# Second-norm shift summed into columns, priority for weight casts, a ninth place for mixer weights, fewer transfers at the opening

## The chip, the core and the metric

One NeuronCore of a Trainium2 chip. The time is the device time of one execution in microseconds (us); the kernel before has a median of 1503.98 us over three runs (1502.64 to 1508.92). Everything is float32 in HBM. The engines are TensorE (PE, its weight loads PEld), VectorE (DVE), ScalarE (ACT), GpSimd (POOL) and SyncE (SP), which here only issues transfers.

## The reference, cut to what matters

A trunk of two layers over 256 tokens of width 1024. Each layer is a mixer (an mLSTM branch and an attention branch, merged and projected) and a mixture of 32 experts of which each token uses two.

```python
for l in range(DEPTH):                                   # 2
    mod = silu(c) @ w_ada[l] + b_ada[l]                  # (1, 6144): six vectors of 1024
    shift1, scale1, gate1, shift2, scale2, gate2 = split(mod, 6)
    h = rms_norm(x, norm1_g[l]) * (1 + scale1) + shift1
    proj = h @ w_in[l] + b_in[l]                         # 1024 x 4880
    ...                                                  # conv, mLSTM, rotary attention, gates
    merged = sigmoid(gm) * (y_m @ w_branch_m[l]) + sigmoid(ga) * (y_a @ w_branch_a[l])
    x = x + gate1 * (merged @ w_out[l])
    h2 = rms_norm(x, norm2_g[l]) * (1 + scale2) + shift2
    x = x + gate2 * hierarchical_moe(h2, ...)            # router, then 32 experts of 3 x 2 MB
return rms_norm(x, final_norm_g)
```

The change turns on `shift2`. It enters twice: as a bias of the router's logits (`shift2 @ w_router`), and as a bias that is added to the gathered tokens of each expert.

## The kernel before, in words

**Weights.** All large weights come in pieces of 1 MB (half a block of 512 columns of `w_in` or `w_ada`, or half an expert matrix) through one list, `plan`, that SP works off in order (`pump`, L151). A piece is sent when a place for it is free. The places are slots of 8 KB per partition: in the mixer four slots of the arena (0, 1, 2, 15) and three tiles `y`, so seven (`usual`), and at the opening of layer 0 four more for `w_ada` alone (`ONCE`). Other slots of the arena hold the mixer's data; late in the mixer they are released one after the other (`free:7:13:14` in the order, L1023, L1078, L1115), and then expert weights go to them too. During the experts all 16 slots and more take expert weights.

**Casts.** The mixer's matmuls run in three passes over operands split into a rounded high part (fp32r) and the rest. For each half block of 256 columns, `prep` (L488) takes a weight piece, casts it on ACT (L495, 128x1024), and subtracts half on DVE and half on POOL (L496, L497, inside `low`, L477). The result goes to one of two spare tiles (three from the merge on). `dense` (L502) first issues the casts for which a spare tile is free, and then 24 matmuls of 256 columns (L535, L550, L523) on the oldest cast weights.

**Order.** PE and SP run in the order of the program (`manual_schedule`). The string `MIX[l]` gives it: a number is so many steps of `dense`, a word is a piece of other work (`dec0` to `dec4` the decays of the mLSTM, `ms` and `mo` its scores and outputs, `as`, `at`, `ao` attention, `kr`, `kt`, `qr`, `qt` the rotary parts). For ACT, DVE and POOL a list scheduler decides the order at build time: among what it takes to be ready, it prefers what the program issues earlier.

**Modulation.** The words `r4` to `r11` and `c0` to `c3` are blocks of 512 columns of `w_ada`, `r` for this layer and `c` for the next. Block b of six pairs: 4, 5 are gate1, 6, 7 are shift2, 8, 9 scale2, 10, 11 gate2; in layer 0 blocks 0 to 3 (`FIRST`: shift1, scale1) open the kernel, in layer 1 blocks 4 and 5 (`EARLY`) open the mixer. `ada_part` (L405) multiplies (L410), casts the partial sums on ACT (L414) and subtracts on DVE (L415); one dense step later `finish` calls `ada_row`, whose two matmuls against a matrix of ones (L442) sum over the partitions and repeat the sum on all 128 of them; DVE adds that to a row tile which holds the bias (L465). For shift2 the row tile is `sh2b`, loaded as a broadcast of 512 KB (L234).

**Where shift2 is turned.** In the middle of the merge, L1062 to L1072 turn one row of `sh2b` into columns: 8 matmuls with one contraction row and two columns (`psh`, L1064; each shows as two records) for the router, with index k outermost, and 8 (`psj`, L1069) with a strided weight read for the experts, with k innermost. L1081 then multiplies the columns with the router weights `wr`.

**Opening.** `setup` (L342) issues `c` and `x` on ACT's queue, the eight pieces of `w_ada` for `FIRST` on SP's, and 13 transfers of small parameters (`params`, L308) on POOL's; one of these, `wg8` (L324), has 1024 runs of 64 bytes. PE then takes two blocks of `FIRST`, transposes x (L664), turns the parameters (L338), turns the blocks' sums (L435), takes the other two blocks, and starts with `dense`.

Of the kernel before, what the change touches and what calls it, by code (L numbers as in the profile page):

```python
# [43 lines left out]
FIRST = (0, 2, 1, 3)  # L44
ORDER = (("q", 2), ("k", 2), ("akv", 1), ("aq", 2), ("v", 2), ("o", 2), ("gm", 4), ("ga", 4))
# [3 lines left out]
    "3 gates 1 gates2 dec0 tables 3 dec1 1 c0 dec2 2 dec3 r5 1 dec4 2 kr 1 qr:0 r11 1 kt 2 qr:1 1 r7 1 hold qt:0 1 ms:0 1 c1 qt:1 2 ms:1 1 as:0 r8 mo:0 mo:1 2 r9 ms:3 1 ms:2 at:0 at:4 r4 as:1 mo:2 1 r10 1 at:1 mo:3 ao:0 at:5 r6 1 ao:2 as:2 mn c2 free:7:13:14 2 mt at:2 1 as:3 2 at:3 c3 at:6 at:7 ao:1 1 ao:3 2",  # L49
    "1 tables 1 gates 2 gates2 dec0 3 dec1 1 dec2 2 dec3 1 dec4 1 kr 2 kt r10 1 qr:0 2 qr:1 r6 1 hold 3 ms:0 qt:1 2 r8 ms:1 1 qt:0 mo:0 as:0 1 r9 mo:1 as:1 1 ms:2 r11 at:0 at:4 ms:3 mo:2 2 at:5 1 at:1 mo:3 ao:0 r7 ao:2 1 as:2 mn free:7:13:14 2 at:2 at:6 1 mt as:3 2 at:3 at:7 ao:1 1 ao:3 2")  # L50
# [4 lines left out]
def trunk(ctx, tc, x, c, w_ada, b_ada, norm1_g, w_in, b_in, conv_w, conv_b, mlstm_norm_g, q_norm_g, k_norm_g,  # L55
# [164 lines left out]
    A2b, sh2b = at(4, 0, D), at(4, D, D)  # L220
# [11 lines left out]
    def late_loads2(l):  # L232
        for t, o in ((g1b, 2), (sh2b, 3), (A2b, 4), (gt2b, 5))[l > 0:]:
# [4 lines left out]
    def first_params():  # L238
        first["p"] = params(0, nc.gpsimd)

    for l in range(depth):
# [5 lines left out]
        for it in stream(l):  # L247
# [60 lines left out]
    def params(l, q):  # L308
# [96 lines left out]
    def ada_part(l, b):  # L405
        pb = ps.tile([P, 512], F32, tag="f", name="pada")
        for h in range(2):
# [4 lines left out]
            done("ada", l, b, h)  # L412
        ph, pw = parts_at[0][:, 0, :], parts_at[0][:, 1, :]
        A.copy(ph, pb)  # L414
        V.tensor_tensor(pw, pb, ph.bitcast(F32), op=ALU.subtract)  # L415
        return ph, pw

    def ada_fast(b):

        pb = ps.tile([P, 512], F32, tag="f", name="pada")  # L420
        for h in range(2):
            w = wt("ada", 0, b, h)
            for kk in range(4):
                T.matmul(pb[32 * kk:32 * kk + 32, :], lhsT=condp[:, 4 * h + kk, :], rhs=w[:, kk, :],
# [1089 lines left out]
```

## Time and profile before

| | |
|---|---|
| median of runs | 1503.98 us (1502.64 to 1508.92) |
| profiled execution | 1508.72 us |
| its span on the core | 1507.0 us, 20322 instructions |
| PE busy | 1358.7 us, 90% |
| PEld, DVE, ACT, POOL busy | 797.8 (53%), 642.6 (43%), 396.0 (26%), 275.9 us (18%) |
| moved by DMA | 522.26 MB, 346 GB/s from and to HBM over the span |

By stage (span of the stage, PE busy, DMA share and rate in it):

| stage | us | PE busy | DMA share | GB/s |
|---|---|---|---|---|
| opening, 0 to 38.95 | 38.95 | 20.18 | 0.98 | 332 |
| mixer of layer 0, to 318 | 279.05 | 254.76 | 0.75 | 264 |
| experts of layer 0, to 771 | 453.00 | 419.17 | 1.00 | 413 |
| mixer of layer 1, to 1047 | 276.00 | 249.74 | 0.64 | 232 |
| experts of layer 1 and end, to 1507 | 460.00 | 414.83 | 0.97 | 401 |

A DMA share near 1 means that all 16 DMA engines of the core have work all the time. A PE that is busy in the table may be busy at half its clock; the column PEclk of the views below tells.

### The profile page before, as it was taken

To read this page: it belongs to the slowest core of one execution; us is meant where nothing else is said; L and a number is where in the kernel's file an instruction comes from. 1 tells how busy PE (TensorE), PEld (TensorE's weight loads), DVE (VectorE), ACT (ScalarE), POOL (GpSimd) and SP (SyncE) were. 2 spreads that over 40 slices of the span, in tenths; PEclk is the share of its full clock that TensorE was granted. 3 is DMA by queue.
4 is the path that set the end of the run, shared out by engine and by line. 5 is a ranking of instruction groups with operands and counts; after the bars stand their busy time and mean duration, and the time that the engine had idled before them with its cause. 6 is when DMAs were issued, how large, how long until landed. Compare 5 with 4: busy or idle time off the path is not lost. (4 is left out here: it accounts for less than half of the span.)

```text
span 1507.0 us, 20322 instructions
## 1 busy us (share of the span) xinstructions
PE 1358.7 (90%) x7902; PEld 797.8 (53%) x7903; DVE 642.6 (43%) x1396; ACT 396.0 (26%) x729; POOL 275.9 (18%) x318
## 2 busy tenths in 40 slices
PE   5899999879999989889978999997999999887996
PEld 2877779834434434334347887994434443334432
DVE  1887664632323312223258867554223323213223
ACT  2536554411111101011035366633111111101101
POOL 4644324500000000000015543550000000000000
PEclk9899999989999999989989999998999999999998
DMA  9877687769999999999995657666999999999995
GB/s 330 314 268 245 245 281 281 275 275 422 420 422 421 420 421 422 420 418 375 416 388 193 227 199 256 224 252 227 422 420 421 422 420 422 421 421 419 378 422 218
DMA packets 122633, 522.26 MB, mean 347 GB/s; under 512 B 14068, under 2 KB 16320, under 8 KB 74400
## 3 DMA queue, kind: packets, MB, share of 16 engines
q1 hardware_dynamic: 116448, 517.00, 86.4%
q0 software_dynamic: 1200, 1.99, 0.7%
q10 hardware_dynamic: 4880, 1.87, 0.5%
q8 instruction: 66, 1.08, 0.3%
q14 instruction: 39, 0.32, 0.1%
HBM read 519.77 MB, written 1.05 MB: 346 GB/s over the span
## 5 line engine op out<-in xcount | busy, mean ns | idle before, releaser
L1268 PE MATMUL pgu<-arena 128*64 128x512 f32 x1456 | 349.3, 595 | 20.5 <-DMA arena<-in_w_up_dram 12.0
L1268 PEld LDWEIGHTS pgu<-arena 128*64 128x64 f32 x1456 | 115.4, 137 | 222.8 <-issue 172.8
L1277 DVE SCALAR_TENSOR_TENSOR arena<-pgu,wsl,arena 128x512 f32<-128x512 f32 x32 | 36.4, 1137 | 383.0 <-PE pgu L1268 383.0
L1293 PE MATMUL pd<-arena 128*64 128x512 f32 x720 | 179.8, 597 | 7.3 <-ACT arena L1284 7.3
L1224 POOL TENSOR_TENSOR arena<-oh,arena 128x256 f32<-128x256 f32 x32 | 19.5, 615 | 740.9 <-DVE oh L1218 468.8
L477 POOL TENSOR_TENSOR R<-arena,R 128x512 fp32r<-128x512 f32 (+1 forms) x84 | 124.9, 1490 | 156.3 <-ACT R L495 104.4
L535 PE MATMUL pd<-R,R 128*128 128x256 f32 x1008 | 134.2, 291 | 9.0 <-DVE R L477 5.7
L550 PE MATMUL pd<-R,R 128*128 128x256 f32 x1056 | 136.4, 288 | 2.2 <-DVE R L477 1.9
L535 PEld LDWEIGHTS pd<-R,R 128*128 128x128 f32 x1008 | 127.1, 197 | 18.4 <-issue 6.9
L550 PEld LDWEIGHTS pd<-R,R 128*128 128x128 f32 x1056 | 130.6, 194 | 8.1 <-issue 4.4
L1304 DVE TENSOR_TENSOR y<-pd,arena 128x512 f32<-128x512 f32 x64 | 44.1, 691 | 204.0 <-PE pd L1293 167.7
L1268 PE MATMUL pgu<-B,arena 128*64 128x512 f32 x432 | 118.0, 594 | 2.7 <-DMA B<-in_w_up_dram 2.7
L477 DVE TENSOR_TENSOR R<-arena,R 128x512 fp32r<-128x512 f32 (+1 forms) x100 | 83.3, 840 | 58.5 <-ACT R L495 53.8
L1293 PEld LDWEIGHTS pd<-arena 128*64 128x64 f32 x720 | 56.0, 138 | 95.3 <-issue 85.5
L1305 ACT CAST yh<-y 128x512 fp32r<-128x512 f32 x64 | 39.6, 619 | 241.9 <-DVE y L1304 241.9
L495 ACT CAST R<-arena 128x1024 fp32r<-128x1024 f32 x76 | 79.4, 1046 | 80.5 <-PE pd L550 26.7
L1316 DVE TENSOR_TENSOR xs<-xs,psc 128x512 f32<-128x512 f32 x128 | 79.3, 680 | 17.9 <-PE psc L1313 17.9
L1240 PE MATMUL pG<-oh,X 128*128 128x256 f32 x512 | 74.3, 309 | 13.2 <-DVE oh L1218 9.0
L1240 PEld LDWEIGHTS pG<-oh,X 128*128 128x128 f32 x512 | 70.8, 215 | 24.2 <-issue 24.2
L1268 PEld LDWEIGHTS pgu<-B,arena 128*64 128x64 f32 x432 | 38.4, 137 | 73.2 <-issue 61.2
L1284 ACT COPY arena<-pat 128x512 f32<-128x512 f32 x32 | 18.7, 585 | 220.1 <-PE pat L1283 220.1
L1244 ACT ACTIVATE arena<-pG,sh2c 128x256 f32<-128x256 f32 x64 | 30.3, 474 | 159.0 <-DVE arena L1246 159.0
(328 smaller groups left out, 1694.4 us busy)
## 6 DMA issues: line engine op xcount, KB each, us to landing
arena<-in_w_up_dram SPq DMA_DIRECT2D x104, 1024.0 KB, 19.8
arena<-in_w_down_dram SPq DMA_DIRECT2D x90, 1024.0 KB, 19.8
arena<-in_w_gate_dram SPq DMA_DIRECT2D x78, 1024.0 KB, 19.8
arena<-in_w_ada_dram SPq DMA_DIRECT2D x36, 1024.0 KB, 6.4
B<-in_w_gate_dram SPq DMA_DIRECT2D x30, 1024.0 KB, 19.8
arena<-in_w_in_dram SPq DMA_DIRECT2D x27, 1024.0 KB, 8.2
B<-in_w_up_dram SPq DMA_DIRECT2D x24, 1024.0 KB, 19.8
X<-in_w_gate_dram SPq DMA_DIRECT2D x20, 1024.0 KB, 19.8
```

Of the source, the lines that this page charges most:

```text
L477: eng.tensor_tensor(dst, full, hi.bitcast(F32), op=ALU.subtract)
L495: A.copy(wh, w)
L535: T.matmul(acc[key][o][:, 0:S], lhsT=w[:, kk, P * o:P * o + P], rhs=x_[:, 4 * kh + kk], start=kh == 0 and i == 0 and kk == 0, stop=kh == 1 ...
L550: T.matmul(acc[key][t][:, 0:256], lhsT=x_[:, 4 * kh + kk, P * t:P * t + P], rhs=w[:, kk], start=kh == 0 and i == 0 and kk == 0, stop=kh == ...
L1240: T.matmul(pG[:, kk, 0:n], lhsT=x_[:, t, k, :], rhs=oh[:, t, :], start=i == 0, stop=i == 3)
L1244: A.activation(xg[k][:, 0:n], pG[:, kk, 0:n], AF.Identity, bias=sh2c[:, k:k + 1])
L1268: T.matmul(pg[CAP * e:CAP * e + CAP, :], lhsT=xg[4 * h + kk][:, P * (i % 2) + CAP * e:P * (i % 2) + CAP * e + CAP], rhs=w[e][:, kk, :], st ...
L1277: V.scalar_tensor_tensor(ac.rearrange("p k q -> p q k"), pu.rearrange("p (q k) -> p q k", k=4), wsl[:, 0:1], sl.rearrange("p (q k) -> p q ...
L1293: T.matmul(pd[n][CAP * e:CAP * e + CAP, :], lhsT=aT[:, 2 * h + kk, CAP * e:CAP * e + CAP], rhs=w[e][:, kk, 512 * n:512 * n + 512], start=h ...
L1304: V.tensor_tensor(y[:, cs], pd, gt2b[:, cs], op=ALU.mult)
L1305: A.copy(yh[:, cs], y[:, cs])
L1316: V.tensor_tensor(xx, xx, pq, op=ALU.add)
```

## The change

1. **Shift2 in columns.** Blocks 6 and 7 no longer go through `ada_part` and `ada_row`. `ada_shift` multiplies as before and copies the partial sums on ACT, reordered, to `turned_sums`; one step later `shift_put` sums over partitions with 8 matmuls whose weights are 64 columns of it, and adds the bias `b3`, straight into the columns `sh2c`. The broadcast of 512 KB, the `psh` and `psj` matmuls and their copies go. The router's bias uses a second copy of the router weights, `wr2`, in the order of `sh2c`, loaded on POOL's queue (runs of 16 and 128 bytes).
2. **Priority for casts.** In `prep` and `ada_part`, cast and subtractions are issued with a priority 60 instructions earlier.
3. **A further place.** A tile `z`, taken first, in each mixer, for all but expert weights and the final norm's gain.
4. **Opening.** The seven transfers of `params` that the first matmuls don't need, and `b3`, move from POOL's queue to SP's list, after the second piece of `w_in` (layer 0 alone). PE transposes x after the first block of `FIRST`, not after the second.
5. **Order.** `dec1` comes one dense step later in both layers; in layer 1 `kt` and some others shift by one too.

```diff
+PREP = 60
-    "3 gates 1 gates2 dec0 tables 3 dec1 1 c0 dec2 2 dec3 r5 1 dec4 2 kr 1 qr:0 ...
-    "1 tables 1 gates 2 gates2 dec0 3 dec1 1 dec2 2 dec3 1 dec4 1 kr 2 kt r10 1 qr:0 2 qr:1 r6 1 hold 3 ms:0 ... 2 at:5 ...
+    "3 gates 1 gates2 dec0 tables 4 dec1 1 c0 dec2 2 dec3 r5 1 dec4 1 kr 1 qr:0 ...
+    "1 tables 1 gates 2 gates2 dec0 4 dec1 1 dec2 2 dec3 1 dec4 1 kr 2 r10 1 kt qr:0 2 qr:1 r6 1 hold 2 ms:0 ... 1 at:4 ... 1 at:5 ...
@@ fits
+        if kind == "z":
+            return key[0] not in ("wg", "wu", "wd", "fin")
@@
-    A2b, sh2b = at(4, 0, D), at(4, D, D)
+    A2b = at(4, 0, D)
+    turned_sums, wr2 = at(4, D, KD, 64), at(4, D + 512, KD, 36)
-        for t, o in ((g1b, 2), (sh2b, 3), (A2b, 4), (gt2b, 5))[l > 0:]:
+        for t, o in ((g1b, 2), (A2b, 4), (gt2b, 5))[l > 0:]:
@@ the list of transfers
+            if l == 0 and it == ("q", 0, 1):
+                add(("more", l), lambda: first["p"]["more"](), None)
@@ params: br (2), wg8, gb, gqk (2) are now in more(q2)
+            b3 = sm.tile([P, KD], F32, tag="b3", name="b3", bufs=1)
+            q2.dma_start(b3, b_ada[l, 3 * D:4 * D].rearrange("(p k) -> p k", k=KD))
@@ setup
+        first_params()
         pump()
-        first_params()
@@ ada_part (ada_sums: the matmuls of L406 to L412)
-        A.copy(ph, pb)
-        V.tensor_tensor(pw, pb, ph.bitcast(F32), op=ALU.subtract)
+        with tc.high_priority(offset=PREP):
+            A.copy(ph, pb)
+            V.tensor_tensor(pw, pb, ph.bitcast(F32), op=ALU.subtract)
+    def ada_shift(l, b):
+        A.copy(turned_sums, ada_sums(l, b).rearrange("p (q k) -> p k q", k=KD))
+    def shift_put(sh2c, b3, b):
+        o = 64 * (b % 2)
+        pc = ps.tile([P, 512], F32, tag="f", name="pshift")
+        for k in range(KD):
+            T.matmul(pc[o:o + 64, 2 * k:2 * k + 2], lhsT=turned_sums[:, k, :], rhs=ones[:, 0:2], start=True, stop=True,
+                     tile_position=(0, o))
+        V.tensor_tensor(sh2c[o:o + 64, :], pc[o:o + 64, 0:2 * KD].rearrange("p (k o) -> p k o", o=2)[:, :, 0],
+                        b3[o:o + 64, :], op=ALU.add)
@@ mixer
+        tiles["z"] = [pool.tile([P, SLOT], F32, name="spare")]
+        free.insert(0, ("z", 0))
@@ prep
-            A.copy(wh, w)
-            low(wl[:, 0:2], w[:, 0:2], wh[:, 0:2], V)
-            low(wl[:, 2:4], w[:, 2:4], wh[:, 2:4], G)
+            with tc.high_priority(offset=PREP):
+                A.copy(wh, w)
+                low(wl[:, 0:2], w[:, 0:2], wh[:, 0:2], V)
+                low(wl[:, 2:4], w[:, 2:4], wh[:, 2:4], G)
@@ opening of layer 0
-            for b in FIRST[:2]:
-                fast[b] = ada_fast(b)
+            fast = {FIRST[0]: ada_fast(FIRST[0])}
         ... (x is transposed here)
             params_cols(p)
+            fast[FIRST[1]] = ada_fast(FIRST[1])
@@ row(b)
+            if b // 2 == 3:
+                ada_shift(l, b)
+                last_sum.append(lambda: shift_put(sh2c, p["b3"], b))
+                return
@@ before the loop over MIX
+        sh2c = sm.tile([P, KD], F32, tag="sh2c", name="sh2c")
+        nc.gpsimd.dma_start(wr2[:, :, 0:4], w_rg[l].rearrange("(p k) g -> p k g", k=KD))
+        nc.gpsimd.dma_start(wr2[:, :, 4:36], w_re[l].rearrange("(p k) g -> p k g", k=KD))
@@ after dense(4)
-        L1062 to L1072: psh, its copy, psj, its copy
-            T.matmul(pL[0][:, 72:108], lhsT=shT[:, k, 0:1].to_broadcast([P, P]), rhs=wr[:, k, :], ...
+            T.matmul(pL[0][:, 72:108], lhsT=sh2c[:, k:k + 1].to_broadcast([P, P]), rhs=wr2[:, k, :], ...
```

## Rows read from the trace of the kernel before

**Rows 1.** Windows: busy us (instructions) of PE, PEld, DVE, ACT, POOL, clock, DMA share, GB/s.

```profile
38.95:318.00 279.05, 254.76 (x1938) 219.39 (x1940) 190.91 (x453) 136.84 (x253) 118.57 (x120) 0.94 0.75 264
318.00:771.00 453.00, 419.17 (x1973) 175.29 (x1969) 126.06 (x212) 53.29 (x96) 9.52 (x20) 0.98 1.00 413
```

**Rows 2.** Window of 5 us where layer 0 passes from mixer to experts, same columns.

```profile
310.00:315.00 5.00, 5.00 (x29) 4.83 (x29) 1.57 (x4) 1.42 (x3) 0.00 (x0) 0.62 0.00 0
```

**Rows 3.** Waits of SP, 0 to 360 us: total us, times, longest.

```profile
SPq L168 <- PE pgu L1268: 32.3, 8, 13.6
```

**Rows 4.** Timeline of PE: start, us, engine, line, operation, output<-inputs, count [idle before <-releaser].

```profile
245.71 1.94 PE L1064 MATMUL psh<-onesr,arena 1*128 1x2 f32 x16
247.52 3.94 PE L1069 MATMUL psj<-onesr,arena 1*128 1x2 f32 x16
251.38 5.04 PE L523 MATMUL pm<-Y,R 128*128 128x256 f32 x24
...
259.14 5.91 PE L523 MATMUL pm<-Y,R 128*128 128x256 f32 x48
```

**Rows 5.** Windows of 5 us in which the clock falls, both mixers.

```profile
65.00:70.00 5.00, 4.26 (x29) 4.26 (x30) 4.78 (x8) 3.05 (x6) 2.89 (x5) 0.80 0.70 228
195.00:200.00 5.00, 5.00 (x21) 2.16 (x24) 1.92 (x5) 0.37 (x1) 0.00 (x0) 0.50 0.02 6
250.00:255.00 5.00, 5.00 (x24) 4.99 (x24) 1.10 (x3) 0.00 (x0) 0.17 (x1) 0.50 0.31 80
850.00:855.00 5.00, 5.00 (x31) 4.91 (x31) 4.28 (x18) 1.05 (x1) 2.00 (x3) 0.69 0.31 85
```

**Rows 6.** Groups by line and shape, whole span: busy, mean ns | idle before, releasers.

```profile
L435 PE MATMUL pcol<-onesr,arena 128*128 128x2 f32 x32 | 3.8, 250 | 0.0
L442 PE MATMUL prow<-part,onesr 128*128 128x512 f32 x40 | 14.9, 430 | 7.6 <-DVE part L415 7.0 <-ACT part L414 0.6
L535 PE MATMUL pd<-R,R 128*128 128x256 f32 x1008 | 134.2, 291 | 9.0 <-DVE R L477 5.7 <-ACT R L495 3.1 <-POOL R L477 0.2
L550 PE MATMUL pd<-R,R 128*128 128x256 f32 x1056 | 136.4, 288 | 2.2 <-DVE R L477 1.9 <-DVE arena L465 0.3
L410 PE MATMUL pada<-arena,condp 128*32 128x512 f32 x248 | 33.4, 644 | 2.9 <-DMA arena<-in_w_ada_dram 2.9
L495 ACT CAST R<-arena 128x1024 fp32r<-128x1024 f32 x76 | 79.4, 1046 | 80.5 <-PE pd L550 26.7 <-PE pd L535 16.9 <-PE pm L523 16.4
```

**Rows 7.** Timeline of PE around the sum of block 6, layer 0.

```profile
191.28 0.39 PE L442 MATMUL prow<-part,onesr 128*128 128x512 f32 x1
...
194.55 0.79 PE L442 MATMUL prow<-part,onesr 128*128 128x512 f32 x1 [2.88 <-DVE part L415]
```

**Rows 8.** Timeline of ACT, DVE and PE at 58 to 66 us.

```profile
58.73 1.03 ACT L495 CAST R<-arena 128x1024 fp32r<-128x1024 f32 x1
60.73 4.27 DVE L567 SCALAR_TENSOR_TENSOR arena<-arena,cols 128x256 f32<-128x256 f32 x8
65.74 1.22 PE L535 MATMUL pd<-R,R 128*128 128x256 f32 x8 [2.58 <-DVE R L477]
```

**Rows 9.** Window in which the convolution runs, layer 0.

```profile
60.00:125.00 65.00, 56.91 (x431) 47.57 (x430) 58.90 (x147) 24.82 (x34) 29.54 (x38) 0.97 0.74 253
```

**Rows 10.** Waits of PE, 700 to 1100 us: the decays of layer 1.

```profile
PE pb L747 <- DVE lf L742: 2.2, 1, 2.2
```

**Rows 11.** Timeline of PE at the opening.

```profile
33.60 1.04 PE L424 MATMUL pada<-arena,condp 128*32 128x512 f32 x8
...
38.95 11.14 PE L535 MATMUL pd<-R,R 128*128 128x256 f32 x72 [2.44 <-ACT R L495]
```

**Rows 12.** Windows of 5 us: small parameters at 10, large pieces at 25, router weights at 220.

```profile
10.00:15.00 5.00, 0.84 (x4) 0.20 (x8) 0.76 (x6) 1.17 (x3) 3.52 (x17) 1.00 0.93 244
25.00:30.00 5.00, 5.00 (x39) 5.00 (x37) 0.26 (x1) 0.00 (x0) 0.35 (x1) 1.00 1.05 387
220.00:225.00 5.00, 5.00 (x42) 2.87 (x42) 4.79 (x6) 4.38 (x7) 2.71 (x2) 1.00 1.09 298
```

More of the change, by code (lines that the diff above doesn't have):

```diff
@@ L44 @@
 FIRST = (0, 2, 1, 3)
+PREP = 60
 ORDER = (("q", 2), ("k", 2), ("akv", 1), ("aq", 2), ("v", 2), ("o", 2), ("gm", 4), ("ga", 4))
 MIX = (
[L49 to L50 removed]
+    "3 gates 1 gates2 dec0 tables 4 dec1 1 c0 dec2 2 dec3 r5 1 dec4 1 kr 1 qr:0 r11 1 kt 2 qr:1 1 r7 1 hold qt:0 1 ms:0 1 c1 qt:1 2 ms:1 1 as:0 r8 mo:0 mo:1 2 r9 ms:3 1 ms:2 at:0 at:4 r4 as:1 mo:2 1 r10 1 at:1 mo:3 ao:0 at:5 r6 1 ao:2 as:2 mn c2 free:7:13:14 2 mt at:2 1 as:3 2 at:3 c3 at:6 at:7 ao:1 1 ao:3 2",
+    "1 tables 1 gates 2 gates2 dec0 4 dec1 1 dec2 2 dec3 1 dec4 1 kr 2 r10 1 kt qr:0 2 qr:1 r6 1 hold 2 ms:0 qt:1 2 r8 ms:1 1 qt:0 mo:0 as:0 1 r9 mo:1 as:1 1 ms:2 r11 at:0 1 at:4 ms:3 mo:2 1 at:5 1 at:1 mo:3 ao:0 r7 ao:2 1 as:2 mn free:7:13:14 2 at:2 at:6 1 mt as:3 2 at:3 at:7 ao:1 1 ao:3 2")
 DENSE = {"q": O_Q, "k": O_K, "akv": O_AK, "aq": O_AQ, "v": O_V, "o": O_O, "gm": O_GM, "ga": O_GA}
@@ L238, in first_params @@
     def first_params():
-        first["p"] = params(0, nc.gpsimd)
+        first["p"] = params(0, nc.gpsimd, nc.sync)
     for l in range(depth):
@@ L412, in ada_part @@
             done("ada", l, b, h)
+        return pb
+    def ada_part(l, b):
+        pb = ada_sums(l, b)
         ph, pw = parts_at[0][:, 0, :], parts_at[0][:, 1, :]
-        A.copy(ph, pb)
-        V.tensor_tensor(pw, pb, ph.bitcast(F32), op=ALU.subtract)
+        with tc.high_priority(offset=PREP):
+            A.copy(ph, pb)
+            V.tensor_tensor(pw, pb, ph.bitcast(F32), op=ALU.subtract)
         return ph, pw
     def ada_fast(b):
[L420 to L424, printed above, removed]
-                         start=h == 0, stop=h == 1, tile_position=(0, 32 * kk))
-            done("ada", 0, b, h)
         t = rot("fast", 5, 0, 2, 512)
-        A.copy(t, pb)
+        A.copy(t, ada_sums(0, b))
         return t
+    def ada_shift(l, b):
[8 more added lines that the diff above has]
+                        b3[o:o + 64, :], op=ALU.add)
     def ada_put(c1, cols, b, t):
@@ L652, in mixer @@
         if l == 0:
-            fast = {}
-            for b in FIRST[:2]:
-                fast[b] = ada_fast(b)
+            fast = {FIRST[0]: ada_fast(FIRST[0])}
         else:
@@ L1061, in mixer @@
         dense(4)
-        ph = ps.tile([P, 512], F32, tag="c", name="psh")
-        for k in range(KD):
-            T.matmul(ph[:, 2 * k:2 * k + 2], lhsT=sh2b[0:1, P * k:P * k + P], rhs=ones[0:1, 0:2], start=True, stop=True)
-        shT = small("shT", KD, 2)
-        V.tensor_copy(shT, ph[:, 0:2 * KD].rearrange("p (k o) -> p k o", o=2))
-        pj = ps.tile([P, 512], F32, tag="c", name="psj")
-        for k in range(KD):
-            T.matmul(pj[:, 2 * k:2 * k + 2], lhsT=sh2b[0:1, :].rearrange("o (q k) -> o k q", k=KD)[:, k, :],
-                     rhs=ones[0:1, 0:2], start=True, stop=True)
-        sh2c = sm.tile([P, KD], F32, tag="sh2c", name="sh2c")
-        V.tensor_copy(sh2c, pj[:, 0:2 * KD].rearrange("p (k o) -> p k o", o=2)[:, :, 0])
         dense(1)
@@ L1080, in mixer @@
         for k in range(KD):
-            T.matmul(pL[0][:, 72:108], lhsT=shT[:, k, 0:1].to_broadcast([P, P]), rhs=wr[:, k, :], start=k == 0,
+            T.matmul(pL[0][:, 72:108], lhsT=sh2c[:, k:k + 1].to_broadcast([P, P]), rhs=wr2[:, k, :], start=k == 0,
                      stop=k == KD - 1)
@@ L1101, in mixer @@
         dump(f"xm{l}", xs)
+        assert not any(r[1][0] == "z" for r in ring.values())
+        free.remove(("z", 0))
         es.close()
```

42 lines of the change are left out of this document (24 added, 18 removed).

## The prediction

> **What bounds the kernel now.** I read the windows by stage first. In the experts all DMA engines are busy (share 1.00 over 453 us) and PE has idle time left; in the mixer of layer 0 the share is 0.75, and PE is busy for 254.76 of 279.05 us, part of that at a lowered clock [rows 1]. So the experts run as fast as their weights come, and the mixers as fast as PE gets through its program. The next question is whether a mixer that ends earlier makes the kernel end earlier. At the passage DMA stands still for a whole window [rows 2], and in SP's waits the longest is for PE's first expert matmuls, 13.6 us [rows 3]: every place is full, and the stream goes on when PE gives places back. From there DMA is the bound to the end of the experts. The start of that stretch hangs on PE, so what PE saves in a mixer is passed on one for one; layer 1 repeats this. The place `z` takes no expert weight, so the number of places filled beforehand stays as it was.
>
> The profiled execution took 1508.72 us (span 1507.0), 4.7 us above the median of the runs shown, 1503.98. The terms are differences inside a mixer, so I take their sum off the median.
>
> **Shift2: what goes.** `psh` starts at 245.71 and the merge goes on at 251.38: 5.67 us of PE for 32 records with two columns [rows 4]. In the window behind them the clock is 0.50, that is the lower of its two levels, 1.2 GHz [rows 5], and the next 24 matmuls of the merge take 5.04 us where 48 later take 5.91, so 2.96 for 24 [rows 4]: 2.08 us more. Together 7.75 us, twice in the kernel: **-15.5 us**. The casts for the merge run beside it, so nothing else waits there; the columns `sh2c` are finished long before the router needs them.
>
> **Shift2: what comes.** Per block the two matmuls of `prow` (14.9 us in 20 blocks, 0.75 each) become 8 matmuls in 16 records. The nearest row is `pcol`, which also sums with two columns: 3.8 us for 32, so 1.9 for 16 [rows 6]. That is 1.15 us more per block, four blocks: **+4.6 us**. Bounds: 0.95 per block if half as many weight columns load in half the time (+0.8 in all), 3.94 if the records go as slowly as `psj` [rows 4] (+12.8). The reordered copy on ACT has a whole dense step, 2.96 us, before `shift_put` needs it; behind `shift_put` on PE waits the whole mixer, so a copy longer than that would cost its excess.
>
> **Block 6 of layer 0.** Its second `prow` matmul waited 2.88 us for DVE's subtraction, which the new form lacks [rows 7]; then a window ran at 0.50, worth 2.5 us [rows 5]. That makes 5.4 us at most. The next thing PE asks for is attention work that DVE and ACT were also late with, so I take **-4.5** (bounds -2.9 and -5.4).
>
> **Priority for casts.** PE waited for cast weights 9.0 us at L535 and 2.2 at L550 [rows 6]; less the 2.44 of the opening [rows 11] and 0.3 for another tile, 8.5 remain. The other `prow` matmuls waited 7.6 - 2.9 = 4.7 us. Two windows behind such waits ran at 0.80 and 0.69, together 5 x (0.20 + 0.31) = 2.6 us [rows 5]. In all 15.8 us. Why they waited is plain at 58 us: the cast ended at 59.76, but DVE then did eight instructions of the convolution for 4.27 us, and its half of the subtraction came behind them, so PE stood 2.58 us [rows 8]. The convolution is not needed for a long while; a priority 60 instructions earlier puts the subtraction ahead. But DVE is busy 58.90 of 65 us there [rows 9]: the work put back must still be done, and some of it becomes the next wait. I take six tenths, **-9.5** (bounds -15.8 and, if order matters nothing, 0; below nothing see the rivals).
>
> **Order.** In layer 1 the decays' matmuls waited 2.2 us for `lf` [rows 10]; one dense step more (2.96 us) covers it: **-2**. The same move in layer 0 I cost at nothing, since no wait stands there now except that for casts, counted above; if the later decays are missed further on, up to one step, 2.96 us.
>
> **Ninth place.** PE waited 2.9 us for pieces of `w_ada` in the mixers (the row of L410) [rows 6], at moments when SP had no place to put them earlier. One place more is one piece of lead; half of it: **-1.5** (0 to -2.9).
>
> **Opening.** In the window from 10 us DMA is full but moves 244 GB/s, against 387 when only large pieces go [rows 12]: (387 - 244)/387 x 5 = 1.85 us are lost to small transfers. Six of them stay, seven move behind two pieces of `w_in`, where the first use, `gates`, comes three dense steps after 38.95, at about 50 us; DMA's lead is large enough to hide them, or else they cost their 1.85 us there. But `wr2` comes on POOL's queue, with 2048 runs of 16 and 128 bytes, and in layer 0 nothing holds it back, so it can be issued in the opening. The like-shaped `wr` was moving in the window at 220 us: 298 GB/s, 1.15 us lost [rows 12]. So the last piece of `FIRST`, which PE finished at 34.64, comes 0.7 us earlier. From there to the first dense step at 38.95 PE waited 2.44 us for the cast [rows 11]; with transposition of x out of the way and the cast ahead, I take half. **-2** (0 to -4.3, all of 1.85 and 2.44).
>
> **Other bytes.** 1.05 MB of broadcasts go and 0.3 MB of `wr2` come; at the 413 GB/s of a full DMA [rows 1] 1.8 us, in stages where DMA is not the bound: nothing.
>
> **Sum.** -15.5 + 4.6 - 4.5 - 9.5 - 2 - 1.5 - 2 = -30.4. All orders on ACT, DVE and POOL are made anew, and where PE now comes sooner some other product will be late; of the waits counted I give back about a fifth of the five reordering terms, 3.4 us. **-27**, from 1503.98 to **1477 us**, own range 1466 to 1488.
>
> **Rivals.**
>
> *The casts' order buys nothing* because DVE, at 91% in that stretch [rows 9], is what PE waits for whichever way it sorts. For it: that share. Against: ACT and POOL have room, and elsewhere DVE is freer. Then +9.5: 1486.
>
> *`shift_put` lowers the clock as `psh` and `psj` do.* For it: two-column matmuls stood before the window at 0.50 [rows 5]. Against: that was 5.67 us of them, and `shift_put` is 1.9. Each of four times would cost the 2.08 us that the merge lost: +8.3, 1485. The Trainium skill, "TensorE: Matmul & The Clock Gate", Part 1, says that the throttled state is the default and activity releases it. [...]
>
> *Casts in front hold their engines; slower than before.* A cast placed ahead that must still wait, for PE to give back the spare tile, holds everything behind it on ACT: decays, exponentials, rotary copies, and PE asks for these in a fixed order. The 76 casts shown stand behind 80.5 us of idle ACT, 1.06 each [rows 6]; one per dense step makes 54 in each mixer, 108. Now that idle time is mostly free, as nothing else was ready. If a third of it reached PE through work held back, 108 x 1.06 / 3 = 38 us: 1515. It decides against the change from 27/108 = 0.25 us per cast. Against it: the scheduler picks among what it takes to be ready, and casts already stand right behind PE. The Trainium skill, same page, "Architectural detail", calls ACT and DVE strict first-in first-out; the row at 58 us agrees, where a finished cast's subtraction sat behind the convolution.
>
> *The mixers' gain is not passed on*, because DMA is the bound after all and only the bytes count: 1502. For it: DMA is full in parts of a mixer and all of the opening. Against: the standstill [rows 2].
>
> **How the numbers follow.** Forecast 0.52; casts buy nothing 0.18; clock 0.12; not passed on 0.06; held engines 0.06; better than the forecast's range, with the whole 15.8 us and the whole opening won, 0.06: about 1463. What a measurement tells from no change is about 0.5%, 7.5 us. Faster by more than that: 0.52 + 0.18 + 0.12 + 0.06 = 0.88, less 0.02 for mixtures of the rivals: 0.86. Within: 0.06 + 0.02 = 0.08. Slower: 0.06. The range takes forecast, casts and clock cases and most of the best one, 1463 to 1494, where the upper end has the casts and clock cases at once (1477 + 9.5 + 8.3).
>
> **What would show it.** Right: no 0.50 window in the merge and some 7.7 us between the same matmuls gone in each mixer; `pshift` groups of 16 records near 1.9 us; waits of L535 and L550 for casts under half of 11.2; no 2.88 us wait near block 6; the first dense step 1 to 4 us before 38.95; expert stretches as long as before (453 us). Wrong: longer waits of PE for decays, scores or attention, more idle DMA in the mixers without PE ending sooner, or a lowered clock behind each `pshift`.

## The result, and the profile after

The changed kernel takes **1494.85 us** (median of 4 runs, 1494.30 to 1495.38) against 1504.64 for the kernel before, measured beside it: ratio 0.9931, 95% interval 0.9909 to 0.9953, some 10 us less where I forecast 27. The time lies just above the range of 1463 to 1494. The profiled execution took 1494.3 us (span 1492.6), clock 0.970.

Windows by stage (busy us and instructions of PE, PEld, DVE, ACT, POOL; clock, DMA share, GB/s). The first answers to the mixer of layer 0, first dense matmul to passage, the second to the experts [rows 1], the third to the standstill of DMA there [rows 2]:

```profile
37.81:306.00 268.19, 246.43 (x1934) 213.24 (x1936) 187.78 (x449) 136.52 (x253) 119.14 (x121) 0.95 0.77 277
318.00:771.00 453.00, 413.63 (x1967) 175.63 (x1967) 132.78 (x237) 58.27 (x107) 12.63 (x23) 0.99 1.01 414
300.00:305.00 5.00, 5.00 (x27) 3.49 (x28) 2.05 (x4) 2.45 (x4) 0.00 (x0) 0.80 0.00 0
```

The mixer is 11 us shorter, and what it saves reaches the end of the experts: `pgu` starts at 302.9 instead of 314.8 us, the first dense matmul of layer 1 at 772.9 instead of 785.5. SP's waits answer to [rows 3]; it still stands up to 13.8 us for PE's places:

```profile
SPq L171 <- PE pgu L1294: 35.1, 9, 13.8
```

The merge, timeline of PE, before and then after (`pm` to `pL`; the rest of before is in [rows 4]):

```profile
234.12 5.92 PE L523 MATMUL pm<-Y,R 128*128 128x256 f32 x48
...
264.89 1.87 PE L1081 MATMUL pL<-arena,shT 128*128 128x36 f32 x16
```

```profile
229.54 5.86 PE L552 MATMUL pm<-Y,R 128*128 128x256 f32 x48
...
252.37 1.87 PE L1105 MATMUL pL<-arena,sh2c 128*128 128x36 f32 x16
```

30.77 us have become 22.83: 7.94 less, where I had 7.75; layer 1 shows 8.0. Block 6 of layer 0, the place of the 2.88 us wait [rows 7]: the sum has no wait, and the next dense step follows 7.93 us after the one before it, where it took 13.66.

```profile
188.92 3.14 PE L564 MATMUL pd<-R,R 128*128 128x256 f32 x24
191.99 1.03 PE L452 MATMUL pshift<-onesr,arena 128*64 128x2 f32 x15
...
196.85 3.14 PE L564 MATMUL pd<-R,R 128*128 128x256 f32 x24
```

The clock's windows answer to [rows 5]; the merge and block 6 are at full clock now, but the opening and the decays of layer 1 are not:

```profile
30.00:35.00 5.00, 5.00 (x23) 3.34 (x24) 0.16 (x1) 0.59 (x1) 0.45 (x5) 0.50 1.08 352
...
195.00:200.00 5.00, 5.00 (x43) 3.56 (x42) 3.64 (x11) 3.30 (x10) 0.00 (x0) 1.00 0.66 223
250.00:255.00 5.00, 5.00 (x46) 5.00 (x45) 3.20 (x7) 2.24 (x4) 3.26 (x4) 1.00 0.31 80
815.00:820.00 5.00, 3.36 (x18) 3.17 (x17) 5.00 (x12) 1.35 (x2) 3.86 (x4) 0.74 0.01 3
```

Groups of PE over the span, as [rows 6]: casts are waited for 7.2 us instead of 9.0 in the first line, not under half, which was to be a sign of being right. The 11.6 us for pieces of `w_ada` all lie in the opening, whose matmuls have the same line now. Before they had a line of their own, L424 below, so 11.6 answers to 16.3 + 2.9, and none of the 2.9 us in the mixers is left. The new `pshift` takes 199 ns a record, 4.4 us for all four blocks:

```profile
L564 PE MATMUL pd<-R,R 128*128 128x256 f32 x1008 | 133.2, 291 | 7.2 <-ACT R L524 4.3 <-DVE R L505 2.6 <-POOL R L505 0.2
L425 PE MATMUL pada<-arena,condp 128*32 128x512 f32 x248 | 33.3, 643 | 11.6 <-DMA arena<-in_w_ada_dram 11.6
L452 PE MATMUL pshift<-onesr,arena 128*64 128x2 f32 x64 | 4.4, 199 | 0.0
```

The line of the kernel before:

```profile
L424 PE MATMUL pada<-arena,condp 128*32 128x512 f32 x40 | 8.8, 967 | 16.3 <-DMA arena<-in_w_ada_dram 16.3
```

PE's waits in layer 1 (total us, times, longest) answer to [rows 10]. The wait for `lf` went from 2.2 to 0.3, as forecast; those for the next two products of the same chain are new:

```profile
PE pa L788 <- DVE al L782: 2.8, 1, 2.8
PE pu L801 <- DVE arena L794: 1.6, 1, 1.6
...
PE pb L775 <- DVE lf L770: 0.3, 1, 0.3
```

The opening [rows 11]: the last piece of `FIRST` is reached 3.7 us earlier, but at half clock `pcol` takes 3.58 us and the first dense step comes only 1.1 us earlier. The wait for the cast is the same 2.44.

```profile
29.93 1.94 PE L425 MATMUL pada<-arena,condp 128*32 128x512 f32 x8 [1.47 <-DMA arena<-in_w_ada_dram]
31.80 3.58 PE L461 MATMUL pcol<-onesr,arena 128*128 128x2 f32 x16
37.81 4.42 PE L564 MATMUL pd<-R,R 128*128 128x256 f32 x19 [2.44 <-ACT R L524]
```

### The profile page after: what moved, and what is told of

Read it like the earlier page. It is cut to its first block, busy times and chain, and to the rows that moved or that the text cites. A ratio compares the mean times of both kernels' runs of the same rounds, so it can differ in the third digit from the quotient of the medians.

```text
span 1492.6 us, 20301 instructions
## 1 busy us (share of the span) xinstructions
PE 1344.6 (90%) x7894; PEld 790.1 (53%) x7895; DVE 640.4 (43%) x1388; ACT 395.0 (26%) x729; POOL 274.8 (18%) x317
## 5 line engine op out<-in xcount | busy, mean ns | idle before, releaser
L1294 PE MATMUL pgu<-arena 128*64 128x512 f32 x1504 | 375.7, 597 | 20.8 <-DMA arena<-in_w_up_dram 14.3
L1294 PEld LDWEIGHTS pgu<-arena 128*64 128x64 f32 x1504 | 124.0, 137 | 243.7 <-issue 186.0
L1319 PE MATMUL pd<-arena 128*64 128x512 f32 x680 | 160.3, 594 | 7.3 <-ACT arena L1310 7.3
L579 PE MATMUL pd<-R,R 128*128 128x256 f32 x1056 | 140.8, 292 | 3.6 <-DVE arena L612 1.4
L564 PE MATMUL pd<-R,R 128*128 128x256 f32 x1008 | 133.2, 291 | 7.2 <-ACT R L524 4.3
L505 POOL TENSOR_TENSOR R<-arena,R 128x512 fp32r<-128x512 f32 (+1 forms) x74 | 110.8, 1501 | 132.3 <-ACT R L524 114.9
L1319 PEld LDWEIGHTS pd<-arena 128*64 128x64 f32 x680 | 50.3, 137 | 95.2 <-issue 84.9
L524 ACT CAST R<-arena 128x1024 fp32r<-128x1024 f32 x66 | 68.8, 1044 | 52.4 <-PE pd L579 23.4
L1310 ACT COPY arena<-pat 128x512 f32<-128x512 f32 x32 | 18.8, 586 | 223.0 <-PE pat L1309 223.0
L1302 ACT ACTIVATE arena<-pgu 128x512 f32<-128x512 f32 x32 | 19.1, 597 | 182.8 <-PE pgu L1294 182.8
```

Of the source, the lines that this page charges most:

```text
L505: eng.tensor_tensor(dst, full, hi.bitcast(F32), op=ALU.subtract)
L524: A.copy(wh, w)
L564: T.matmul(acc[key][o][:, 0:S], lhsT=w[:, kk, P * o:P * o + P], rhs=x_[:, 4 * kh + kk], start=kh == 0 and i == 0 and kk == 0, stop=kh == 1 ...
L579: T.matmul(acc[key][t][:, 0:256], lhsT=x_[:, 4 * kh + kk, P * t:P * t + P], rhs=w[:, kk], start=kh == 0 and i == 0 and kk == 0, stop=kh == ...
L1294: T.matmul(pg[CAP * e:CAP * e + CAP, :], lhsT=xg[4 * h + kk][:, P * (i % 2) + CAP * e:P * (i % 2) + CAP * e + CAP], rhs=w[e][:, kk, :], st ...
L1319: T.matmul(pd[n][CAP * e:CAP * e + CAP, :], lhsT=aT[:, 2 * h + kk, CAP * e:CAP * e + CAP], rhs=w[e][:, kk, 512 * n:512 * n + 512], start=h ...
```

## The experiments

Each was timed in five rounds beside the kernel before. Ratios are to that kernel; 0.001 is 1.5 us. A difference of two ratios is good to some 0.0025, worked out from their intervals.

### The parts alone, and the priority taken away

Theory A: the priority only moves waits, from casts to what the casts pass on a full DVE. Theory B was my prediction's: it removes them.

**no_priority**, the changed kernel without (shortened):

```diff
-        with tc.high_priority(offset=PREP):   # in ada_part and in prep
```

> The changed kernel with the casts and subtractions at their ordinary priority; all else as changed. Theory A (the priority gives nothing: it moves the wait from casts to decays, sums and rotary parts, because the same VectorE does all of them): 1488 to 1495 us, so as fast as the changed kernel or up to 7 us faster, and the waits of TensorE for the decays of layer 1 (2.77 and 1.64 us) gone. Theory B (the priority is worth the 9.5 us predicted, and something else took them back): 1500 to 1505 us.

Measured: 1489.03 us, 0.9895 (0.988 to 0.991). The priority costs the changed kernel 0.0036, 5.4 us, good to some 4.

**shift_only**, the kernel before with part 1 of the change alone (`ada_shift`, `shift_put`, `b3`, `wr2`).

> The kernel before with the first part of the change alone: shift2 summed into columns, second copy of the router weights; old order, old opening, seven places, ordinary priority. Theory A (this part holds the whole gain, about 8 us in each merge, 5 at block 6, less 2 for the new sums): 1484 to 1490 us, faster than the whole change. Theory B (the parts add up as predicted and the shift's own gain is smaller, by the 10 to 14 us that are missing): 1494 to 1500 us.

Measured: 1491.11 us, 0.9900 (0.9885 to 0.9916), that is -15.1 us, between the ranges of its two theories. My terms for it were -15.5 + 4.6 - 4.5 = -15.4. It carries a loss of its own in the opening (first dense step at 41.4 instead of 38.2 to 39 us) with `wr2` on POOL's queue beside the other small transfers.

**priority_only**, the kernel before with part 2 alone.

> The kernel before with priority 60 for casts and subtractions alone. Theory A (waits are moved, not removed): 1501 to 1510 us, within 0.5% of the kernel before. Theory B (worth what was predicted): 1493 to 1497 us, with TensorE's waits for cast weights under 5 us in place of 11.

Measured: 1514.88 us, 1.0061 (1.0046 to 1.0077): 9 us slower, more than either theory allowed. **before_again** is the kernel before, unchanged, as the yardstick of the traces: 1507.48 us, 1.0005 (0.9996 to 1.0015).

> The kernel before once more, for a second trace: the profiled execution of it took 4.7 us more than the median of its runs. Theory A (that execution drew longer waits of TensorE in the mixers than others do; the excess is in the windows behind them at the lower clock): 1502 to 1506 us, with the passage to the experts of layer 0 some 2 us earlier than 314.8, or that of layer 1 earlier than 1041.8. Theory B (the excess is in the experts or at the end): the passages at the same times.

In layer 1 the waits of PE in priority_only are these; before_again has 2.2 for `lf`, 0.2 for the scan and 0.6 at `pkt`, and 2.2 each for DVE's casts at L535 and for the parts, which have fallen to nothing and 0.6 here:

```profile
PE pb L750 <- DVE lf L745: 3.2, 1, 3.2
PE ppt L958 <- DVE arena L950: 2.7, 4, 1.1
...
PE pu L776 <- DVE arena L769: 2.0, 1, 2.0
PE pkt L844 <- DVE arena L819: 1.5, 1, 1.5
```

All are products of DVE. Behind them the clock falls; in the window 775 to 850 us it is 0.89 against 0.94 in before_again:

```profile
775.00:850.00 75.00, 66.76 (x493) 60.19 (x493) 54.72 (x143) 33.72 (x50) 40.02 (x50) 0.89 0.63 223
```

So A holds in kind: the casts came earlier, as meant, and what they passed came later. Layer 1 takes 90.1 us from its first dense step to its first scores, against 85.7 in before_again. **part_only** keeps the priority in `ada_part` and takes it from `prep`.

> The changed kernel with the priority kept for the parts of the block sums (ada_part) and taken from the casts of weights (prep). If the casts of weights make the loss (theory A: 27 casts in a mixer up to the scores, each with 0.68 us or more on DVE, pass the decays): as without any priority, a ratio of 0.988 to 0.991 to the kernel before. If the parts do (few, but each passes at its block): 0.992 to 0.994, as the changed kernel.

Measured: 1491.09 us, 0.9900 (0.9883 to 0.9917). The loss sits in `prep`, with the casts of weights; the difference from the changed kernel, 0.0031, is only just clear of the intervals.

**decays_too** puts the decays, which the casts pass, under the same priority (shortened):

```diff
         def dec0():   # and dec1 to dec4
+            with tc.high_priority(offset=PREP):
```

> The changed kernel with the decays' own instructions (dec0 to dec4) put under the same priority as the casts, so that casts no longer pass them. Theory A (the priority is paid for by the decays: casts overtake the chain lf, al, scan, and PE waits for those instead, 2.8 us for al and 1.6 us for the scan in layer 1 and 2.5 us of half clock behind them): the waits at pa and pu go back under 1 us each, the layer 1 mixer up to its first scores gets 4 to 6 us shorter (changed kernel 90.0 us), and the time is 1488 to 1491. Theory C (it does not matter who is displaced: DVE is full there, so the wait only moves on to rotary, sums or the casts again): 1493 to 1497, with the same sum of waits under other names.

Measured: 1486.81 us, 0.9867 (0.985 to 0.9884), 9.6 us better than the changed kernel by the ratios. The wait for `al` is 1.1 instead of 2.8 us, that for the scan is gone. The windows from the first dense step of layer 1 to its first scores, in the changed kernel, decays_too and no_priority:

```profile
772.90:862.90 90.00, 80.81 (x630) 74.00 (x627) 68.69 (x167) 38.73 (x55) 49.08 (x60) 0.92 0.68 236
768.70:854.20 85.50, 78.06 (x631) 71.04 (x628) 68.38 (x167) 38.92 (x55) 48.74 (x60) 0.96 0.71 248
768.20:858.40 90.20, 79.76 (x631) 72.36 (x627) 69.10 (x167) 39.18 (x55) 46.90 (x60) 0.94 0.69 239
```

So the decays pay for the casts in this stretch, and putting them first wins 4.5 us there. But without any priority the stretch is as long, with PE waiting for casts:

```profile
PE pd L562 <- ACT R L522: 4.0, 2, 3.2
...
PE pd L577 <- DVE R L504: 1.5, 2, 0.9
...
PE pd L562 <- DVE R L504: 1.2, 1, 1.2
```

Here the priority took away all but 0.7 of 6.7 us of waits for casts and brought 4.7 for the decays, at a lower clock, 0.92 against 0.94. The 7.6 us between the two profiled executions lie elsewhere: 2.4 in the opening, and 4.8 behind the first scores of the two layers, where PE's waits differ by little. What makes those isn't shown.

### Order, place, opening

All on the kernel without the priority (0.9895).

**order_back** has the `MIX` strings of the kernel before.

> The kernel without the priority (1489.0), with the written order of the mixers of the kernel before. If the new order buys what I predicted (2.2 us wait of layer 1's decays gone): 1491, with a wait of some 2 us at pb in layer 1 back. If the order only had worth beside the priority, or none: 1489, with the waits for decays merely moved between pb, pa and pu.

Measured: 1485.91 us, 0.9868 (0.9849 to 0.9886). The new order is no gain; by the ratios it costs about 4 us, only just clear of the intervals. In the old order PE waits 2.1 for `lf` and 2.2 for a cast before the decays of layer 1; in the new one, asking for one cast more by then, it waits 4.0 + 1.2 for casts. **decays_order**, the changed kernel with decays first and this order, came to 1485.94 us, 0.9855 (0.9837 to 0.9873), between its two expectations: the gains overlap at least in part.

> The changed kernel with the decays under the same priority as the casts (ratio 0.9867) and the written order of the kernel before (worth 0.0027 without the priority). If both remove different waits: 0.983 to 0.985. If the order's worth was the same wait for casts that the priority removes: 0.986 to 0.989, and the two seconds-best versions stand for the same optimum.

**place_back** drops the tile `z`.

> The kernel without the priority (1489.0), without the ninth place z. If a place more gives lead as I predicted (1.5 us of waits of pada for pieces of w_ada): 1490 to 1491, with idle time at pada up by 1 to 3 us in the mixers. If the pieces come in time anyway: 1489 and the same idle time at pada.

Measured: 1497.53 us, 0.9933 (0.992 to 0.9946): the place is worth 0.0038, 5.7 us, four times my term. Timeline of SP, without the place and then with it: SP can ask for the 17th transfer from `w_in` only at 168.81 instead of 157.57 us, and pieces of `w_ada` stand behind it. PE then waits 2.80 and 1.44 us for two of those, in the third block below.

```profile
168.81 0.37 SPq L171 DMA_DIRECT2D arena<-in_w_in_dram  x1
```

```profile
157.57 0.37 SPq L171 DMA_DIRECT2D arena<-in_w_in_dram  x1
```

```profile
178.34 1.06 PE L425 MATMUL pada<-arena,condp 128*32 128x512 f32 x8 [2.80 <-DMA arena<-in_w_ada_dram]
180.84 1.93 PE L425 MATMUL pada<-arena,condp 128*32 128x512 f32 x8 [1.44 <-DMA arena<-in_w_ada_dram]
```

Between 60 and 200 us the largest of SP's waits, 55.1 of some 126 us, is for places that a cast's subtraction gives back (`R`). But between 150 and 170 us it waits for `pada` (11.0) and for transfers of `w_ada` to land (8.0), so that the place covers late casts is likely and not shown.

**wr2_later** loads `wr2` from SP's list, behind the second late loads.

> The kernel without the priority (1489.0), with the two transfers of wr2 moved from POOL's queue at the start of a mixer to SP's list behind the second late loads. Theory (wr2's 2048 small runs in the opening hold up the last pieces of w_ada there, and PE waits): first dense step 2 to 3 us before 35.4, and the time 1486 to 1488; layer 1 unchanged. Rival (the opening is bound by something else, the transposes of x and the cast chain): first dense step within 0.5 us of 35.4 and the time 1489, or later if the small runs hold up pieces of w_in on SP's list in the mixer.

Measured: 1488.70 us, 0.9875 (0.9859 to 0.9891). First dense step at 34.1 instead of 35.4 us; the gain of some 3 us is within the intervals.

**more_pool** issues the small parameters on POOL's queue instead of SP's list; **more_pool_noz** also drops the place; **opening_back** has the opening of before.

> The kernel without the priority (1489.0), in which the small parameters that the opening puts on SP's list between pieces of w_in (from 23.8 to 36.5 us on SP, behind which DMA falls to 15 to 45 GB/s at 35 to 38 us) go out on POOL's queue instead, at the same place in the program. Theory D (the opening's change costs as much as it gains, since SP's list stands behind the small transfers and the lead in weights is lost): DMA stays above 300 GB/s from 33 to 40 us, the mixer of layer 0 gets 2 to 4 us shorter, 1485 to 1487. Rival (the lead comes back before anything waits for it, as I had predicted): the standstill goes, the time stays at 1488 to 1490.

> The same without the ninth place. If the 8.5 us that the ninth place was worth in the run without it (1497.5 against 1489.0) come from the lead lost in the opening, the place is worth 1 to 3 us here: 1487 to 1490. If they come from the late casts themselves, which give places back late (SP waited 55 us for casts between 60 and 200 us, and a piece of w_in was asked for at 168.8 instead of 157.6 us), PE waits some 4 us for w_ada at 175 to 183 us again, and the time is 1493 to 1498.

> The kernel without the priority (1489.0), with the opening of the kernel before: small parameters all on POOL's queue behind the first pieces, the second block of FIRST taken before the transposes of x; wr2 stays. If the opening is worth the 2 us that I predicted: 1491, first dense step 38 to 41 against 35.4 us. If its gain is given back by the lead lost (theory D): 1487 to 1489, though the first dense step is later by 3 to 5 us, with the difference made good before the first scores (126.4 us).

Measured: more_pool 1492.04 us, 0.9899 (0.9883 to 0.9914); more_pool_noz 1500.74, 0.9958 (0.9945 to 0.9972); opening_back 1493.58, 0.9902 (0.9887 to 0.9918). Theory D fell: DMA no longer falls back at 35 to 40 us (396 GB/s instead of 171 in no_priority), but the transfers were issued in the opening again, the first dense step came at 40.6 instead of 35.4 us, and nothing was gained. The lead lost on SP's list cost nothing that shows. The opening itself is worth 0.0007, 1 us, by the ratios, and 4.6 us by the first dense steps (40.0 against 35.4); my 2 lies between. The pair with and without the place gives 8.9 us for it, so its worth doesn't come from the opening. In the traces of both pairs it is one stretch, from the first scores of layer 0 to the merge: 106.2 and 105.7 us without the place, 99.6 with it.

**best1** joins the old order, priority for the decays alone, and both moves of transfers: 1487.76 us, 0.9869 (0.9854 to 0.9884). Nothing added up.

> The kernel without priority for the casts, but with the priority on the decays alone, the written order of the kernel before, wr2 behind the second late loads and the small parameters on POOL's queue: the four findings together. If they add: 1485.9 (order) less 1 to 2 for the decays, 0 to 1 for wr2 and 0 to 3 for the small parameters, 1480 to 1484. If each only moves the same waits: 1485 to 1488.

### Why DVE is late

Five kernels of other orders ended between 0.9855 and 0.9875, each with other waits, nearly all for DVE. The groups of the cast's subtraction in the kernel before (line L477, busy us, mean ns) hold a clue that I had not looked at: the same shape takes 896 or 974 ns on DVE when POOL does the other half, but 684 ns where one input is in PSUM and POOL has no part (`Y<-pyt`, `part<-pada`):

```profile
L477 DVE TENSOR_TENSOR R<-arena,R 128x512 fp32r<-128x512 f32 x76 | 68.1, 896 | 54.1 <-ACT R L495 53.8
L477 DVE TENSOR_TENSOR R<-B,R 128x512 fp32r<-128x512 f32 x22 | 21.4, 974 | 4.7 <-ACT R L495 4.6
L415 DVE TENSOR_TENSOR part<-pada,part 128x512 fp32r<-128x512 f32 x20 | 13.7, 686 | 8.3 <-ACT part L414 8.1
...
L477 DVE TENSOR_TENSOR Y<-pyt,Y 128x512 fp32r<-128x512 f32 x4 | 2.6, 684 | 0.5 <-ACT Y L923 0.5
```

And in the changed kernel, timeline of DVE and of POOL at 58 to 63 us: one instruction of the convolution, 0.47 us elsewhere, takes 3.31 us and ends 0.3 us after the second of two subtractions on POOL. The decays' first instruction (L767) comes behind it.

```profile
58.45 0.68 DVE L505 TENSOR_TENSOR R<-arena,R 128x512 fp32r<-128x512 f32 x1
59.06 3.31 DVE L596 SCALAR_TENSOR_TENSOR arena<-arena,cols 128x256 f32<-128x256 f32 x1
...
62.90 0.47 DVE L596 SCALAR_TENSOR_TENSOR arena<-arena,cols 128x256 f32<-128x256 f32 x1
63.29 0.16 DVE L767 SCALAR_TENSOR_TENSOR ab<-gt 128x16 f32<-128x16 f32 x1
```

```profile
59.53 1.29 POOL L505 TENSOR_TENSOR R<-arena,R 128x512 fp32r<-128x512 f32 x1
...
60.80 1.27 POOL L505 TENSOR_TENSOR R<-arena,R 128x512 fp32r<-128x512 f32 x1
```

It looks as if DVE stood still while POOL works, with its row counting that as busy. A late half of POOL's own is not the cause: PE waited 0.2 us for it [rows 6]. The Trainium skill, "SBUF — State Buffer", "Who interferes with whom", says that a DVE instruction with two SBUF inputs contends with a GpSimd instruction that reads SBUF, and that the loser blocks and doesn't share. These rows agree. That the one that starts first has its way, as that page says too, they neither show nor refute: the 3.31 us begin 0.47 us ahead of POOL's, but the times of POOL's rows are rough.

**no_pool** is the kernel without the priority, and with POOL out of `prep`; **no_pool_prio** is the changed kernel with the same edit; **before_no_pool** is the kernel before with this one line and no part of the change.

```diff
-            low(wl[:, 2:4], w[:, 2:4], wh[:, 2:4], G)
+            low(wl[:, 2:4], w[:, 2:4], wh[:, 2:4], V)
```

> The kernel without the priority (ratio 0.9895) with both halves of a cast's subtraction on DVE, none on POOL. Theory P (DVE's waits come from its standing still while POOL subtracts: 0.68 us alone, but 1.0 us on average and up to 3.65 us beside POOL): DVE's subtractions all take about 0.68 us, and the 0.68 us more for each of some 54 casts of a mixer are made up by what no longer stretches: ratio 0.983 to 0.990. Theory L (DVE is late by its plain load): 37 us more of DVE in each mixer, 16 of them before the first scores, where it has some 18 us free: PE waits 5 to 12 us more in each mixer, ratio 0.996 to 1.006.

> The changed kernel, priority and all (ratio 0.9931), with both halves of a cast's subtraction on DVE. Theory P: the priority's loss was POOL's subtractions drawn beside DVE's work, so it goes: ratio 0.983 to 0.991. Theory A and L (casts ahead of decays on a full DVE): still more DVE work ahead of the decays, ratio 1.000 to 1.012, with waits for al, the scan and the rotary tables above those of the changed kernel (2.8 and 1.6 us).

> The kernel before with both halves of a cast's subtraction on DVE and nothing else changed. Theory P (PE waited for casts and parts in the kernel before because DVE stood still beside POOL's subtractions): the waits that I had counted there go without any priority, ratio 0.975 to 0.985, as the same edit made of 0.9895 a 0.9718. Rival (the edit only pays together with the new order, place and opening, whose lead it uses): ratio 0.990 to 1.000.

| kernel | us | ratio | interval |
|---|---|---|---|
| no_pool | 1463.58 | 0.9718 | 0.9704 to 0.9732 |
| no_pool_prio | 1479.93 | 0.9826 | 0.9812 to 0.984 |
| before_no_pool | 1477.55 | 0.9813 | 0.9789 to 0.9836 |

Theory L falls in all three: more work on DVE made the kernel faster. Theory P holds in kind. In before_no_pool its size is right too; no_pool gained more than it said, 0.9718 against 0.983 at best; for no_pool_prio it had the priority's loss go with POOL, and that didn't come true (below). By the ratios the edit takes 28 us off the kernel before (1477.55 against 1504.45), as much as I had forecast for the whole change, and 27 us off the kernel without the priority. The window 60 to 125 us, the kernel without the priority and then no_pool: DVE does 161 instructions instead of 139 in the same busy time, where POOL does 14 fewer, and PE gets 62.83 us of work done instead of 57.86, at full clock.

```profile
60.00:125.00 65.00, 57.86 (x457) 49.71 (x458) 54.53 (x139) 25.71 (x34) 29.32 (x33) 0.97 0.83 292
```

```profile
60.00:125.00 65.00, 62.83 (x511) 53.07 (x510) 54.41 (x161) 31.05 (x44) 11.93 (x19) 1.00 0.94 339
```

The mixer of layer 0 in before_no_pool, the window that answers to [rows 1]:

```profile
38.81:301.16 262.35, 246.73 (x1938) 215.65 (x1940) 193.03 (x507) 136.69 (x253) 38.69 (x66) 0.95 0.79 281
```

In before_no_pool the group of subtractions has twice the instructions at 758 ns instead of 896. The group that writes `Y`, with both inputs in SBUF, goes from 1243 ns, the first line, to 687:

```profile
L477 DVE TENSOR_TENSOR Y<-arena,Y 128x512 fp32r<-128x512 f32 x10 | 12.4, 1243 | 6.8 <-ACT Y L495 6.8
```

```profile
L477 DVE TENSOR_TENSOR R<-arena,R 128x512 fp32r<-128x512 f32 x152 | 111.3, 758 | 48.1 <-ACT R L495 46.7 <-PE pxa L1052 1.1
L477 DVE TENSOR_TENSOR Y<-arena,Y 128x512 fp32r<-128x512 f32 x20 | 13.0, 687 | 4.4 <-ACT Y L495 4.4
```

So the shorter time is not a matter of an input in PSUM: DVE's instruction is blocked beside POOL's, which the clue above had only suggested.

And the priority costs even more there: no_pool_prio is 16 us slower than no_pool, so its loss there comes from the order of the work, not from POOL's subtractions being drawn forward.

**best2** adds the old order, the decays' priority and the later `wr2` to no_pool.

> The kernel without priority for casts and with both halves of a subtraction on DVE (ratio 0.9718), with the written order of the kernel before, the priority on the decays alone and wr2 behind the second late loads. Left of waits there are 2.8 us for casts in layer 0, 1.8 us for al and 2.2 us for casts in layer 1, some 2 us of the opening, and the step of 2.96 us that the old order sets earlier costs nothing: ratio 0.968 to 0.971 if the edits go with one another, 0.971 to 0.974 if they only move what is left.

Measured: 1470.34 us, 0.9766 (0.9741 to 0.9792): slower than no_pool, outside both expectations. The timelines of ACT and PE show one place that lost 6.79 us: with the decays ahead, ACT goes back and forth between their functions and the convolution's, loads a table four times (1.28 us each) and brings the cast late. no_pool has four such loads too, from 55.91 to 64.59 us, but there a pair of casts stands ahead of them, at 53.47.

```profile
54.24 1.28 ACT L769 ACT_TABLE_LOAD   x1
...
59.02 1.28 ACT L598 ACT_TABLE_LOAD   x1
...
60.64 1.98 ACT L524 CAST R<-arena 128x1024 fp32r<-128x1024 f32 x2
```

```profile
61.72 7.35 PE L564 MATMUL pd<-R,R 128*128 128x256 f32 x48 [6.79 <-ACT R L524]
```

The best kernel of the study is therefore no_pool, 0.972 of the kernel before.

## Why the prediction was wrong

- **What bounds the kernel, and that a mixer's gain is passed on**: right, 1 to 1 through the experts.
- **Shift2 goes and comes, block 6**: the mechanism is right. That -15.4 predicted meets -15.1 measured alone is in part luck. In the changed kernel the merges gave 15.9 us where I had 15.5. `pshift` took 1.1 us for 16 records instead of 1.9 and lowered no clock, so the rival on that fell, and what comes cost 1.4 instead of 4.6. Block 6 gave 5.7, a little above my upper bound of 5.4. That makes -20.2; 2 to 3 us of it went in the opening of shift_only, and where the rest went isn't worked out.
- **Priority for casts, -9.5: the step that failed.** It cost 5.4 us in the changed kernel and 9 alone, so some 15 of the 17 us that I missed. The prediction said that DVE's convolution is not needed for a long while and that six tenths of 15.8 us of waits would go. Waits for casts did go, 6.0 us of them in the first stretch of layer 1. But the casts passed not only the convolution but also the decays and the rotary parts, which PE asks for within a step or two: 4.7 us of waits for the decays and a lower clock came instead, and the stretch took 90.0 us with the priority and 90.2 without. I had seen that DVE is busy 58.90 of 65 us [rows 9] and took four tenths off for it; the whole gain went. That the priority even costs time is shown by its ratios, though some of the 5.4 us may be the clock in the opening (see there). In priority_only the waits named here explain a part, as they lengthen this stretch by 4.4 us; in the changed kernel the place of the net loss is known and its cause stays open. My rival with that mechanism, "the casts' order buys nothing", stopped at zero, and the one on the other side looked for the loss on ACT instead of DVE.
- **The reading of [rows 9]** is what lay under it: part of the 58.90 us is DVE standing still. The cure was the place of the work, not its order: in before_no_pool the waits at L535, at L550 and for the sums fall from 18.8 to 7.3 us, those for DVE's and ACT's casts at L535 in layer 0 from 5.8 to the 2.4 of the opening. It gains more than these waits: of the 16.7 us that the mixer of layer 0 gets shorter, 8.7 are idle time of PE, and the other 8.0 are the same 1938 matmuls done in less time.
- **Order, -2**: the wait for `lf` went as forecast, 2.2 to 0.3 us, and came back as waits for casts and, with the priority, for `al` and the scan; taken away without the priority, it gave about 4 us back. The term's sign was wrong.
- **Ninth place, -1.5**: 5.7 and 8.9 us in two comparisons. I had counted waits for `w_ada` in the trace of before; its worth shows in waits that appear when it is taken away.
- **Opening, -2**: 1 us by the ratios and 4.6 by the first dense steps without the priority, the latter just above my bound of 4.3. In the profiled run of the changed kernel half of it was lost to the half clock at 30 to 40 us. That is no effect of the priority: place_back, which has none, runs the same `pcol` at half clock, and its first dense step stands at 37.80 us. The cast's 2.44 us did not shrink.
- **The range**: its upper end was 1477 + 9.5 + 8.3 = 1494.8, written as 1494. That the time comes so near to it is luck, since neither `pshift`'s clock nor a priority worth nothing is what happened. Its lower end, 1463, is 2 us lower than its terms give, 1465.

The single terms add to between -12 us (shift -15.1, place -5.7, opening -1, order +4, priority +5.4) and -19 (with 8.9 and 4.6 for place and opening), against the -10 measured: they may cover each other's waits, and the account of which gave what has this much play. Not tried: keeping PE busy in the opening so that its clock stays up, and moving POOL's subtractions to ACT.

## What to carry to other kernels

When an engine is busy for nine tenths of a stretch, ask first what its instructions take there against the same shape elsewhere: a mean above the shortest is time that another place for the work may win. Before you put one product forward on a shared engine, list what it passes and when each of these is asked for; if the list is as urgent as the product, the waits move and the time need not fall. An edit's worth as one more place or one more step of lead shows only by taking it away, since the waits it covers aren't in the trace.

## What the runs showed of the hardware

- A DVE subtraction with two inputs in SBUF stands still beside a subtraction on POOL: 0.68 us alone (the median in no_pool), 0.9 to 1.2 on the average of a group beside it in the kernel before, up to 3.65 us in no_priority.
- In the opening of the changed kernel PE waited 1.36 and 1.47 us around eight matmuls, and the clock was 0.50 in the 5 us window behind; 16 `pcol` records then took 3.58 us instead of 1.95. In no_pool, with waits of 1.37 and 1.49 us at the same places, the eight matmuls behind still took 1.06 us, as at full clock, and `pcol` 2.56. So waits like these were not enough by themselves to bring it down there. `pshift`, also with two columns, left it at 1.00 at block 6.
- Alternating functions on ACT cost a table load of 1.28 us for each change in best2, in a stretch where PE stood 6.79 us for a cast.
